# Newton steps of the residual norms moved to GpSimd, and two modulation chunks tied to the second norm of layer 1

## The chip, the cores and the metric

The kernel runs on one core of a Trainium2 chip. The metric is the device time of one execution in microseconds. The core's engines work side by side, each through its own queue in order: TensorE (PE, its weight loads shown apart as PEld), VectorE (DVE), ScalarE (ACT), GpSimd (POOL), and SyncE (SP), which here issues the loads from memory.

## The reference, cut to what matters

Two transformer stacks of two layers each run one after the other on 256 tokens of width 1024, all in float32. The first stack (with a second stream of 256 context tokens) has adaptive layer norms: six modulation vectors per layer come out of a product of the condition with `w_ada`. The change touches the root-mean-square norms and when two parts of that product run:

```python
def rms_norm(x, g):
    xf = x.astype(jnp.float32)
    y = xf * lax.rsqrt(jnp.mean(xf * xf, axis=-1, keepdims=True) + NORM_EPS)
    return (y * g.astype(jnp.float32)).astype(x.dtype)

def adaln(cond, w_ada, b_ada):
    m = jax.nn.silu(cond) @ w_ada + b_ada
    return jnp.split(m, 6, axis=-1)
```

In a layer of the first stack the residual after attention is normed, scaled and shifted by modulation vectors, and goes through a gated feed-forward, `(silu(h @ w_gate) * (h @ w_up)) @ w_down`.

## The kernel before

Activations lie transposed, channels on the 128 partitions in eight tiles (k = 0 to 7) and tokens along the free axis, 256 for each stream. Every float32 weight block of 128 x 128 is split into a rounded part (`whi`, a cast on ScalarE, L210) and a residual (`wlo`, a subtraction on VectorE, L211), the activations likewise (names ending in h and l), and `mm3` makes three matmuls of each product (L336 to L338).

Weights come through a ring of three raw buffers of 1 MB each (tag `raw`), loaded from SP's queue: L203 for the split weights, L487 for modulation weights, which are used unsplit. A load can be issued only when a buffer has been released: a split weight's by its last residual, a chunk's by its matmuls. The loads of SP's queue are issued in order.

A modulation chunk is one of the 12 parts of a layer's `w_ada`: `ada_chunk(l, c)` issues two loads, makes the matmuls of both halves (L494; the second half's buffer is read first), copies the result (L503), transposes it (L505) and reduces it on VectorE (L508, L509). The matmuls are built in `together`, which raises their priority by 3000 and makes the first of them follow the chunk's loads in the planned order. The chunks (1,10) and (1,11) are built behind the modulation of layer 1's second norm, but being of high priority they are planned as soon as their loads allow.

A residual norm goes as follows. The output projection (L336 to L338 into `dn`) adds to the residual stream tile by tile (L711), each tile is squared (L384) and added up (L388). `sum_cols` sums over the partitions with two matmuls against ones (L357), `mean_eps` makes the mean (L362), and `rsqrt` finds the inverse root: two integer instructions for a first guess (L345, L346) and three Newton rounds of three instructions (L348 to L350), all on VectorE with 2 elements in each partition (4 in one case). `spread` turns the result into a row over all partitions with two transposes (L369), ScalarE copies it (L523 or L933), and the modulation (L535 to L537) or the split of the activations follows.

`rsqrt` is called for: the first norm of all (L794), `norm_row` for both streams in layer 0's feed-forward norm, for both at the end of layer 0, and for the one stream in layer 1's feed-forward norm, `row_stats` twice at the start of the layers of the second stack (L917 on), the head norms (`head_rms`), and the final norm. `row_stats` at its first call has 4 columns.

Around the second norm of layer 1 the order of work is: the output projection in two parts, the column sums, the norm, and the feed-forward's first pair of weights (four column groups of 24 matmuls each, 96 in all). A planner sets the order on each engine from priorities, dependencies and its estimates of durations; on the chip each engine keeps that order. A dependency of class NoSync sets the order only.

Of the kernel before, what the change touches and what calls it, by code (L numbers as in the profile page):

```python
# [13 lines left out]
ALU = mybir.AluOpType  # L14
# [4 lines left out]
P = 128  # L19
KT = 8  # L20
D = 1024
# [234 lines left out]
class Build:  # L256
# [82 lines left out]

    def rsqrt(self, v, n, name):  # L340

# [3 lines left out]
        nc.vector.tensor_scalar(y.bitcast(I32), v.bitcast(I32), 1, None, op0=ALU.logical_shift_right)  # L345
        nc.vector.tensor_scalar(y.bitcast(I32), y.bitcast(I32), -1.0, float(0x5F376800), op0=ALU.mult, op1=ALU.add)  # L346
        for _ in range(3):
            nc.vector.tensor_tensor(t, y, y, op=ALU.mult)  # L348
            nc.vector.scalar_tensor_tensor(t, t, -0.5, v, op0=ALU.mult, op1=ALU.mult)
            nc.vector.scalar_tensor_tensor(y, t, 1.5, y, op0=ALU.add, op1=ALU.mult)  # L350
        return y

    def sum_cols(self, acc, n, ps=None):

        ps = self.bank("tr") if ps is None else ps
        for j in range(n):
            self.link(self.nc.tensor.matmul(ps[:, j:j + 1], acc[:, j * P:(j + 1) * P], self.ones, start=True, stop=True))  # L357
        return ps[:, :n]
# [6 lines left out]
    def spread(self, r, n):  # L365

        ps = self.bank("tr")
        for j in range(n):
            self.link(self.nc.tensor.transpose(ps[:, j * P:(j + 1) * P], r[:, j:j + 1].to_broadcast([P, P]), self.ident))  # L369
        return ps[:, :n * P]  # L370
# [97 lines left out]

    def ada_chunk(self, l, c, tag="mm"):

        raws, loads = self.ada_load(l, c, self.wp, "raw", self.raw_bufs)
        ps = self.bank(tag)
        with self.together(loads) as add:
            for i in (1, 0):
# [44 lines left out]
    def norm_row(self, s):  # L519

        rb = self.acc[:, s * 256:s * 256 + 256]
        v = self.mean_eps(self.sum_cols(rb, 2), 2, D, "ms")
        self.nc.scalar.copy(rb, self.spread(self.rsqrt(v, 2, "rn"), 2))  # L523
        return rb
# [211 lines left out]
    def block1(self, ctx):  # L736
# [61 lines left out]
        for l in range(2):  # L798
# [48 lines left out]
            with tc.tile_pool(name=f"ffn{l}", bufs=1, reuse_waits="tile") as fp:  # L847
                h = self.parts(fp, "F")
                for st in apart:
# [8 lines left out]
                    self.modulate(h, self.norm_row(st[0]), l, 1, st[0])  # L858
                    for a in self.ada_gap[l]:
                        self.ada_chunk(*a)  # L860
                f0 = 0
# [53 lines left out]
    def row_stats(self, acc, first):  # L915
# [3 lines left out]
        if first is None:  # L919
            r = self.rsqrt(self.mean_eps(self.sum_cols(acc, 2), 2, D, "ms2"), 2, "rr")  # L920
        else:
# [5 lines left out]
            nc.vector.scalar_tensor_tensor(v[:, 2:4], self.sum_cols(acc, 2), 1.0 / D, t, op0=ALU.mult, op1=ALU.add)  # L927
            r = self.rsqrt(v, 4, "r4")
            r1, r = r[:, 0:2], r[:, 2:4]
# [351 lines left out]
```

## Time and profile before

| | us |
|---|---|
| median of 3 runs | 1557.29 (1557.05 to 1558.81) |
| the profiled execution | 1557.46 |
| its span, first to last instruction | 1555.7 |
| mean granted clock of TensorE in the span | 0.991 |
| TensorE busy | 1498.9 |
| VectorE busy | 1003.9 |
| ScalarE busy | 800.9 |
| GpSimd busy | 67.2 |

Busy times are sums over the span; the ends of matmuls are modelled. The clock is given as a share of the full 2.4 GHz.

### The profile page before, as it was taken

Reading aid. Unit: us, or ns where it says so; the run is one execution under the profiler, and the core shown is the slowest. Engines: PE = TensorE matmul, PEld = TensorE weight load, DVE = VectorE, ACT = ScalarE, POOL = GpSimd, SP = SyncE. Lnnn points to the kernel's source line nnn. Section 1 sums busy time; section 2 is a strip of 40 time slices with the busy share of each in tenths; the row PEclk is TensorE's granted clock in tenths of the full one; section 3 lists DMA queues with packets and bytes.
Section 4 is the critical chain, followed back from the end, with each engine's and each line's share of the span. In section 5 each row is a group of like instructions: output and inputs, shape, how many; then the busy total and the mean of one; then the engine's idle time right before and its main releaser. Section 6 shows DMA issues by size and latency. Waiting matters only on the chain.

```text
span 1555.7 us, 25050 instructions
## 1 busy us (share of the span) xinstructions
PE 1498.9 (96%) x9826; PEld 1291.0 (83%) x9826; DVE 1003.9 (65%) x2210; ACT 800.9 (51%) x1499; POOL 67.2 (4%) x83
## 2 busy tenths in 40 slices
PE   5999999999999999999899999999999999999997
PEld 2776689787788789856599999898899999899996
DVE  4674688333233336867565556898767779987775
ACT  3466665222222224567554445677665456776542
POOL 0200000000000000010000000102100010201000
PEclk9999999999999999999999999999999999999998
DMA  9313355424322524353845554434435544334451
GB/s 370 122 55 115 138 200 187 162 86 158 135 92 98 190 81 139 132 212 109 308 166 189 181 175 168 153 111 160 153 127 184 178 149 156 136 109 163 164 175 42
DMA packets 36982, 238.36 MB, mean 153 GB/s; under 512 B 4224, under 2 KB 5888, under 8 KB 15104
## 3 DMA queue, kind: packets, MB, share of 16 engines
q1 hardware_dynamic: 36576, 236.14, 42.9%
q8 instruction: 77, 1.26, 0.3%
q0 software_dynamic: 288, 0.62, 0.2%
q14 instruction: 41, 0.34, 0.1%
HBM read 236.32 MB, written 1.05 MB: 153 GB/s over the span
## 4 chain that ended last, share of the span: by engine, by line
PE 82%; DVE 10%; ACT 3%; DMA 2%; issue 2%; POOL 0%; SPq 0%; ACTq 0%; POOLq 0%; DVEq 0%
PE mm L336 11%; PE mm L337 10%; PE mm L338 10%; PE g L337 6%; PE g L336 6%; PE g L338 6%; PE dn L337 5%; PE dn L338 5%; PE dn L336 5%; DVE wlo L211 3%; PE mm L494 2%; PE tr L632 2%; PE pv L640 2%; PE pv L996 1%; PE mx L336 1%
## 5 line engine op out<-in xcount | busy, mean ns | idle before, releaser
L210 ACT CAST whi<-raw 128x1024 fp32r<-128x1024 f32 (+4 forms) x392 | 370.0, 949 | 495.3 <-PE mm L337 137.5
L211 DVE TENSOR_TENSOR wlo<-raw,whi 128x1024 fp32r<-128x1024 f32 (+4 forms) x392 | 431.1, 1104 | 198.1 <-ACT whi L210 196.3
L337 PE MATMUL dn<-Hl,whi 128*128 128x256 f32 (+1 forms) x520 | 161.7, 311 | 0.0
L338 PE MATMUL dn<-Hh,wlo 128*128 128x256 f32 (+1 forms) x520 | 161.1, 310 | 0.1
L336 PE MATMUL dn<-Hh,whi 128*128 128x256 f32 (+1 forms) x520 | 160.7, 310 | 0.0
L336 PE MATMUL mm<-Hh,whi 128*128 128x256 f32 (+1 forms) x512 | 149.4, 292 | 1.0 <-DVE mod L508 0.7
L338 PE MATMUL mm<-Hh,wlo 128*128 128x256 f32 (+1 forms) x512 | 150.0, 293 | 0.0
L337 PE MATMUL mm<-Hl,whi 128*128 128x256 f32 (+1 forms) x512 | 149.4, 292 | 0.0
L336 PE MATMUL mm<-whi,Hh 128*128 128x384 f32 (+2 forms) x352 | 129.2, 367 | 0.0
L338 PE MATMUL mm<-whi,Hl 128*128 128x384 f32 (+2 forms) x352 | 127.3, 362 | 0.0
L337 PE MATMUL mm<-wlo,Hh 128*128 128x384 f32 (+2 forms) x352 | 127.2, 361 | 0.0
L336 PE MATMUL mm<-Fh,whi 128*128 128x256 f32 (+1 forms) x368 | 123.0, 334 | 1.7 <-ACT Fh L536 1.7
L338 PE MATMUL g<-Fh,wlo 128*128 128x256 f32 (+1 forms) x368 | 123.0, 334 | 0.3 <-DVE wlo L211 0.3
L336 PE MATMUL g<-Fh,whi 128*128 128x256 f32 (+1 forms) x368 | 122.5, 333 | 0.0
L337 PE MATMUL g<-Fl,whi 128*128 128x256 f32 (+1 forms) x368 | 122.4, 333 | 0.0
L337 PE MATMUL mm<-Fl,whi 128*128 128x256 f32 (+1 forms) x368 | 122.2, 332 | 0.0
L338 PE MATMUL mm<-Fh,wlo 128*128 128x256 f32 (+1 forms) x368 | 122.2, 332 | 0.0
L337 PEld LDWEIGHTS dn<-Hl,whi 128*128 128x128 f32 x520 | 99.1, 191 | 8.3 <-issue 2.5
L338 PEld LDWEIGHTS dn<-Hh,wlo 128*128 128x128 f32 x520 | 99.1, 191 | 6.0 <-issue 0.8
L336 PEld LDWEIGHTS dn<-Hh,whi 128*128 128x128 f32 x520 | 99.0, 191 | 5.6 <-ACT whi L210 0.4
L336 PEld LDWEIGHTS mm<-Hh,whi 128*128 128x128 f32 x512 | 97.9, 191 | 2.2 <-ACT whi L210 0.8
L338 PEld LDWEIGHTS mm<-Hh,wlo 128*128 128x128 f32 x512 | 97.9, 191 | 1.6 <-issue 0.8
(284 smaller groups left out, 3240.2 us busy)
## 6 DMA issues: line engine op xcount, KB each, us to landing
raw<-in_w_ada_dram SPq DMA_DIRECT2D x48, 1024.0 KB, 4.9
raw<-in_w_gu_dram SPq DMA_DIRECT2D x44, 1024.0 KB, 4.9
raw<-in_w_mix_dram SPq DMA_DIRECT2D x32, 1024.0 KB, 4.8
raw<-in_w_in_dram SPq DMA_DIRECT2D x40, 768.0 KB, 4.3
raw<-in_w_in_dram SPq DMA_DIRECT2D x20, 1024.0 KB, 4.8
raw<-in_w_dn_dram SPq DMA_DIRECT2D x16, 1024.0 KB, 4.8
raw<-in_w_dn_dram SPq DMA_DIRECT2D x12, 768.0 KB, 4.3
raw<-in_w_out_dram SPq DMA_DIRECT2D x8, 1024.0 KB, 4.9
```

What stands on the lines that cost most here:

```text
L210: nc.scalar.copy(hi[:, :m], x)
L211: nc.vector.tensor_tensor(lo[:, :m], x, hi[:, :m].bitcast(F32), op=ALU.subtract)
L336: self.link(nc.tensor.matmul(out, lhs[0], rhs[0], start=start, stop=False))
L337: self.link(nc.tensor.matmul(out, lhs[0], rhs[1], start=False, stop=False))
L338: self.link(nc.tensor.matmul(out, lhs[1], rhs[0], start=False, stop=stop))
L494: made.append(self.nc.tensor.matmul(ps[32 * g:32 * g + 32, :], self.s32[:, 4 * i + g, :], raws[i][:, 512 * g:512 * g + 512], start=i == fi ...
L632: nc.tensor.transpose(ps[:, (2 * j + qt) * P:(2 * j + qt + 1) * P], p[i][:, qt, c:c + P], self.ident)
L640: first(nc.tensor.matmul(pv[i * 64:i * 64 + 64, :256], v, pts[i][0][:, j * 256:j * 256 + 256], start=b == 0 and j == 0, stop=b == nk // 2 ...
L996: f(nc.tensor.matmul(pv[64 * i:64 * i + 64, c], vs[i][j], pt[:, d], start=first and j == 0, stop=last and j == 1))
```

## The change

`rsqrt` gets a flag `aside`. With it the first guess stays on VectorE, and the three Newton rounds go to GpSimd, four instructions each instead of three, as GpSimd does the product with v and the step -0.5 x + 1.5 one after the other. `norm_row` and `row_stats` set the flag, which makes seven calls: both streams of layer 0's feed-forward norm, both at the end of layer 0, layer 1's feed-forward norm, and both layers of the second stack.

`sum_cols` and `spread` keep their last matmul and transpose in `self.summed` and `self.turned`. `ada_chunk` takes further instructions that the first of its matmuls has to follow in the order; in layer 1, chunk (1,10) follows the last column sum and chunk (1,11) the last transpose.

```diff
-    def rsqrt(self, v, n, name):
+    def rsqrt(self, v, n, name, aside=False):
...
+        if aside:
+            for _ in range(3):
+                nc.gpsimd.tensor_tensor(t, y, y, op=ALU.mult)
+                nc.gpsimd.tensor_tensor(t, t, v, op=ALU.mult)
+                nc.gpsimd.tensor_scalar(t, t, -0.5, 1.5, op0=ALU.mult, op1=ALU.add)
+                nc.gpsimd.tensor_tensor(y, y, t, op=ALU.mult)
+            return y
         for _ in range(3):
...
-            self.link(self.nc.tensor.matmul(ps[:, j:j + 1], acc[:, j * P:(j + 1) * P], self.ones, start=True, stop=True))
+            self.summed = self.nc.tensor.matmul(ps[:, j:j + 1], acc[:, j * P:(j + 1) * P], self.ones, start=True, stop=True)
+            self.link(self.summed)
...
-            self.link(self.nc.tensor.transpose(ps[:, j * P:(j + 1) * P], r[:, j:j + 1].to_broadcast([P, P]), self.ident))
+            self.turned = self.nc.tensor.transpose(ps[:, j * P:(j + 1) * P], r[:, j:j + 1].to_broadcast([P, P]), self.ident)
+            self.link(self.turned)
...
-    def ada_chunk(self, l, c, tag="mm"):
+    def ada_chunk(self, l, c, tag="mm", after=()):
...
-        with self.together(loads) as add:
+        with self.together(loads + list(after)) as add:
...
-        self.nc.scalar.copy(rb, self.spread(self.rsqrt(v, 2, "rn"), 2))
+        self.nc.scalar.copy(rb, self.spread(self.rsqrt(v, 2, "rn", True), 2))
...
-                    for a in self.ada_gap[l]:
-                        self.ada_chunk(*a)
+                    for a, behind in zip(self.ada_gap[l], (self.summed, self.turned)):
+                        self.ada_chunk(*a, after=[behind])
...
-            r = self.rsqrt(self.mean_eps(self.sum_cols(acc, 2), 2, D, "ms2"), 2, "rr")
+            r = self.rsqrt(self.mean_eps(self.sum_cols(acc, 2), 2, D, "ms2"), 2, "rr", True)
...
-            r = self.rsqrt(v, 4, "r4")
+            r = self.rsqrt(v, 4, "r4", True)
```

## Rows read from the trace of the kernel before

**Rows 1.** The page, part 1: busy us, share of the span, instructions

```profile
PE 1498.9 (96%) x9826; PEld 1291.0 (83%) x9826; DVE 1003.9 (65%) x2210; ACT 800.9 (51%) x1499; POOL 67.2 (4%) x83
```

**Rows 2.** Windows: stretch, length, busy us and count by engine, PE's clock, DMA

```profile
25.00:30.00 5.00, 1.12 (x5) 0.70 (x5) 3.94 (x11) 2.65 (x5) 0.00 (x0) 0.73 1.01 419
...
770.00:775.00 5.00, 2.11 (x17) 1.64 (x16) 4.29 (x12) 3.94 (x6) 0.00 (x0) 0.98 0.90 380
775.00:780.00 5.00, 0.37 (x2) 0.29 (x2) 4.28 (x12) 1.55 (x2) 0.00 (x0) 0.50 1.01 342
780.00:785.00 5.00, 3.48 (x17) 3.19 (x16) 4.27 (x11) 3.04 (x7) 0.00 (x0) 0.50 0.22 92
```

**Rows 3.** Timeline of PE around layer 1's second norm: start, duration us, line, tiles

```profile
760.91 1.92 PE L494 MATMUL mm<-raw,s 128*32 128x512 f32 x16 [0.36 <-DMA raw<-in_w_ada_dram]
...
767.51 1.92 PE L494 MATMUL mm<-raw,s 128*32 128x512 f32 x16
...
769.58 0.28 PE L338 MATMUL dn<-Hh,wlo 128*128 128x256 f32 x1
...
770.29 0.28 PE L338 MATMUL dn<-Hh,wlo 128*128 128x256 f32 x1
...
772.97 0.60 PE L357 MATMUL tr<-ones,acc 128*128 128x1 f32 x4 [1.96 <-DVE acc L388]
...
779.63 0.66 PE L369 MATMUL tr<-ident,rn 128*128 128x128 f32 x2 [5.56 <-DVE rn L350]
...
781.81 0.58 PE L336 MATMUL mm<-Fh,whi 128*128 128x256 f32 x1 [1.52 <-ACT Fh L536]
...
782.41 0.42 PE L336 MATMUL mm<-Fh,whi 128*128 128x256 f32 x1
782.62 0.41 PE L337 MATMUL mm<-Fl,whi 128*128 128x256 f32 x1
```

**Rows 4.** Timeline of SP's queue in the same stretch: issues of loads

```profile
762.03 0.33 SPq L487 DMA_DIRECT2D raw<-in_w_ada_dram  x1
762.89 0.33 SPq L203 DMA_DIRECT2D raw<-in_w_gu_dram  x1
...
768.63 1.19 SPq L203 DMA_DIRECT2D raw<-in_w_gu_dram  x2
```

**Rows 5.** Timeline of VectorE and ScalarE in the same stretch

```profile
771.36 1.22 DVE L211 TENSOR_TENSOR wlo<-raw,whi 128x1024 fp32r<-128x1024 f32 x1
...
772.50 0.42 DVE L388 TENSOR_TENSOR acc<-acc,sq 128x256 f32<-128x256 f32 x1
...
773.51 1.99 ACT L210 CAST whi<-raw 128x1024 fp32r<-128x1024 f32 x2 [0.49 <-DMA raw<-in_w_gu_dram]
...
776.00 1.04 ACT L210 CAST whi<-raw 128x1024 fp32r<-128x1024 f32 x1 [0.50 <-DMA raw<-in_w_gu_dram]
```

**Rows 6.** Timeline: Newton steps in layer 0's norm, and GpSimd's smallest product

```profile
252.04 0.16 DVE L348 TENSOR_TENSOR rn_t<-rn 128x2 f32<-128x2 f32 x1
...
253.60 0.16 DVE L350 SCALAR_TENSOR_TENSOR rn<-rn_t,rn 128x2 f32<-128x2 f32 x1
...
6.17 0.20 POOL L768 TENSOR_TENSOR g<-vec 128x8 f32<-128x8 f32 x1 [4.22 <-DMA vec<-in_vec_dram]
```

**Rows 7.** Timeline of GpSimd and VectorE where both work, near 209 us

```profile
209.08 0.82 DVE L211 TENSOR_TENSOR wlo<-raw,whi 128x640 fp32r<-128x640 f32 x1
209.16 0.93 POOL L730 TENSOR_TENSOR tq<-c,row 128x64 f32<-128x64 f32 x1 [102.42 <-DMA row<-in_row_dram]
...
210.06 0.32 POOL L730 TENSOR_TENSOR tk<-c,row 128x64 f32<-128x64 f32 x1
```

**Rows 8.** Timeline of PE at the spread before the second stack's second layer

```profile
1264.54 0.36 PE L336 MATMUL mm<-whi,Hh 128*128 128x452 f32 x1
1264.73 0.36 PE L337 MATMUL mm<-wlo,Hh 128*128 128x452 f32 x1
1265.19 0.40 PE L369 MATMUL tr<-ident,rr 128*128 128x128 f32 x2
```

## The prediction

> **What bounds the kernel now.** I read the busy shares first: the tensor engine works in 96% of the span, VectorE in 65%, GpSimd in 4% [rows 1]. So nearly everything that keeps PE's queue from moving costs its own length, and what is taken off VectorE or put on GpSimd costs nothing unless PE ends up waiting for it. Next I looked for the stretch where PE is not busy. The windows by stage show one inside the kernel [rows 2]: between 770 and 785 us PE works 2.11, 0.37 and 3.48 us out of 5.00 each, and its granted clock stands at 0.50, the lower of its two levels (1.2 GHz instead of 2.4), from about 775 to 785. This is the second norm of layer 1. The timeline of PE there [rows 3] gives its parts: the two modulation chunks (1,10) and (1,11) run at 760.91 and 767.51 in the middle of the output projection, the projection's last product starts at 770.29, the column sums of the norm at 772.97, the spread at 779.63, the first product of the feed-forward at 781.81. The other six norms that the change touches sit in stretches where PE is always busy; there only a late spread can cost anything.
>
> **Chunks in layer 1's gap: the path shortens.** In the order before, the two chunks stand ahead of the sums. Each holds PE for 1.92 us, and the first waited 0.36 us for its load: 2 x 1.92 + 0.36 = 4.2 us [rows 3]. With the new dependencies chunk (1,10) may only follow the last column sum and chunk (1,11) only the last transpose of the spread, so the projection's last product starts near 766.1. The sums follow it by 2.7 us today, of which some 0.9 us is the addition L388 waiting behind a weight residual of 1.22 us on VectorE [rows 5]; that weight would not yet be loaded (next part), so the wait goes. Sums: 772.97 - 4.2 - 0.9 = 767.9; end of the sums near 768.5.
>
> **The load ring: what is late next.** The raw buffers are three, and feed-forward weights come through them behind the chunks. Rows of SP's queue show the chain [rows 4]: the fourth chunk load is issued at 762.03, when half of the first chunk is multiplied, the first feed-forward load at 762.89, at its end; the next two at 768.63 and 769.49 (two issues of 0.33 us within 1.19), at half and end of the second chunk. So holding the chunks holds these loads, and everything behind them on SP's queue. Chunk (1,10) would now run 768.5 to 770.4. The fourth chunk load is issued near 769.5, the first feed-forward load near 770.4. For two loads issued 0.86 us apart the rows of casts give the landing: the loads of 768.63 and 769.49 released their casts at 773.51 and 776.00, 4.9 and 6.5 us later [rows 4, 5]. Hence the chunk's load lands at 774.4, the feed-forward weight at 776.9, its cast takes 1.0 us, two of them 1.99 [rows 5], and the first feed-forward product can start at 778.0. The norm's own chain must be done before that: 768.5, three VectorE instructions of 0.2 ahead of the steps [rows 6], twelve Newton instructions on GpSimd 2.4 to 2.9 (below), and from the spread to the first product the 2.2 us of today, 779.63 to 781.81 [rows 3]: about 774. The weight, not the norm, ends last, with 4 us to spare, which hides GpSimd's part here. Chunk (1,11) runs 774.4 to 776.3, in PE's wait, and frees the loads for the third and fourth column group: landing 4.9 us after 775.4 is 780.3, both casts and the first residual done near 782.6. The first two groups hold PE for 48 products x 0.12 us (six spacings between 769.58 and 770.29 [rows 3]) = 5.8 us, to 783.8, so that is just covered; if the cover fails, each us of delay is a us lost.
>
> **What it is worth.** The first weight pair is 96 products. Before: 15 of them started by 785.0 at half clock (17 instructions in that window, two of them transposes), 81 remained at 0.12 us, end 794.7 [rows 2, 3]. After, at full clock: 778.0 + 96 x 0.12 = 789.5. That is 5.2 us. **Clock:** it fell about 4 us after the projection's last dense work, with two short bursts of 0.6 us between, and at the start of the kernel too, where PE was busy 1.12 us of 5.00 [rows 2]. After the change the longest thin stretch is 770.4 to 774.4, with only the spread in it. No row shows whether chunks of 1.92 us suffice to hold the clock. Bounds: nothing lost, or the 15 products at 0.21 instead of 0.12 twice over, 2.7 us [rows 3]. I take one such spell, 15 x 0.09 = 1.4 us, since the nearest row, the present gap, shows a fall after a stretch no emptier. Gap: -5.2 + 1.4 = -3.8 us.
>
> **Newton steps on GpSimd.** Seven calls lose 9 VectorE instructions each and gain 12 on GpSimd, because the fused instruction becomes two. On VectorE alone the nine take 252.04 to 253.76, 1.7 us, 0.19 us each [rows 6]; taking 63 of them away is worth nothing by itself, VectorE being in no path there. The smallest GpSimd product on record, 128x8, took 0.20 us [rows 6]; for 128x2 I take 0.20 to 0.24, so a chain of 2.4 to 2.9 us undisturbed. What comes on top is the wait for VectorE: a GpSimd product of 128x64 that began 0.08 us after a residual took 0.93 us, and the same form without neighbour 0.32 [rows 7]: it was held until the residual had finished, 0.6 us. Residuals and additions of that kind stand in VectorE's queue in five norms (not in layer 0's feed-forward norm of the second stream, nor now in layer 1's). PE is in order: the spread's transposes have a fixed place, and behind them queue the products that PE could otherwise run; the row copy of ScalarE and the modulations wait for the transposes, but with slack. Today PE waits only about 0.25 us there: products at 1264.54 and 1264.73, transposes at 1265.19, where 0.20 would be the spacing [rows 8]. Bounds for the five together: -1.2 us (all of today's waits gone) to +8 us (each chain 0.7 longer than nine VectorE steps, plus a hold of 0.6 to 1.2, 1.6 us x 5). I take +0.4 us: the present order meets the end of such a chain within some 0.3 us [rows 8], so the planner's times are good, and the GpSimd chain leaves a VectorE queue in which the steps had to take turns with residuals anyhow. Both ends stay in the range.
>
> A rule speaks against the move. The Trainium skill, Perfetto Trace Analysis, Optimizing Scalar/DVE Operations, says that GpSimd and VectorE share an SBUF read port, held as a lock by a two-port VectorE instruction, so that moving work between the two might not help. By that rule the +8 end would be the nearer one; [rows 7] agree that such holds exist, but not how often twelve small steps meet one.
>
> **Sum.** Profiled execution: 1557.46 us (span 1555.70, 1.76 around it; the median of the runs is 1557.29). 1557.46 - 3.8 + 0.4 = **1554.1 us**.
>
> **Rivals.** (a) The gap stays weight-bound: PE's order puts products of the third or fourth column group early, as the mixed order before does, and PE waits for their residual at 782.6. Then only about 24 products are done by then, 72 remain: end 791.2 at full clock, 2.0 more with the clock low; gain 1.4 to 3.4, less 0.4: near 1556. For it: the buffers hold only three loads and the new waits stand at the head of SP's queue. Against: the order is planned with the landing times in view, and the first chunk waited only 0.36 us for its load today [rows 3]. (b) **Slower:** PE waits for GpSimd. In the five norms whose spread stands among dense products the transposes come into PE's queue where an undisturbed chain would end, while VectorE's residuals hold GpSimd. At 1.6 us each the loss is 8 us: 1557.46 - 3.8 + 8 = 1561.7. It decides from 0.75 us a norm on, where 5 x 0.75 eats the gap's 3.8. For it: [rows 7], and PE's 96%. Against: GpSimd has nothing else to do before the chain, being busy 4% of the span [rows 1], and VectorE's nine steps met the same residuals in their own queue. (c) The hold does not act as told: the chunk's load is late, the clock falls as before and the feed-forward starts at half clock near 781: 1557, no change.
>
> **How the numbers follow.** A change under 0.2% (3.1 us) can't be told from none here. Forecast, the gap gained and the other norms neutral: 0.42, with a range of its own of 1551.0 to 1554.3. Rivals (a) and (c), and mild forms of (b): 0.32, within 3.1 us. Rival (b) in full: 0.26. The range reaches from the gap at full clock with today's waits gone, 1557.46 - 5.2 - 1.2 = 1551.0, to (b), 1561.7.
>
> **What would show it.** Right: in the trace after, both chunks lie between the sums and the first feed-forward product, sums near 768, first product near 778, landing of a weight as its releaser. The clock around 775 tells the 1.4 us. Wrong: PE idle ahead of the transposes, released by GpSimd, of 1 us or more in the layer-0 norms, at 980 or at 1265; GpSimd steps of much over 0.25 us spacing; PE waiting for a residual inside the first weight pair; an extra loss in the output projection, if something other than the chunks held it.

## The result and the profile after

| | before | after |
|---|---|---|
| median of the runs shown | 1557.29 us (1557.05 to 1558.81) | 1580.0 us (1573.95 to 1580.79) |
| ratio | | 1.0127, 95% interval 1.0116 to 1.0138 |
| profiled execution, span | 1557.46 us, 1555.70 us | 1574.94 us, 1573.2 us |

The change makes the kernel 1.3% slower; 1554.1 us was forecast, with a range up to 1561.7. The runs of after lie in two groups, near 1574 us (mean granted clock 0.988 and 0.991) and near 1580 us (0.986 and 0.987); the profile is of the first, and no trace here shows the second. The ratio is not the quotient of the two medians, which is 1.0146; that of the means of the runs shown is 1.0131.

The page's part 1, to be held against [rows 1] (busy us, share of the span, instructions):

```profile
PE 1504.6 (96%) x9826; PEld 1294.0 (82%) x9826; DVE 997.0 (63%) x2147; ACT 801.1 (51%) x1499; POOL 88.3 (6%) x167
```

VectorE is 6.9 us less busy, GpSimd 21 us more, and PE's work grew by 5.7 us with the same 9826 instructions, which points to stretches at the lower clock. The difference of the spans, 17.5 us, is mostly time in which PE stood still (17.5 less 5.7: 11.8 us). The waits of PE say for whom (who <- for whom: us in total, times, longest):

```profile
PE tr L377 <- POOL rn L352: 10.8, 5, 4.2
PE tr L377 <- DVE rr L940: 4.2, 2, 2.6
```

L377 are the spread's transposes, L352 is the last instruction of a Newton round on GpSimd, and L940 is VectorE's small copy behind the steps in the second stack. In before the transposes waited more than 0.1 us in one norm of these seven, layer 1's [rows 3]. The timeline of PE at the seven norms (start, us, engine, line, operation, tiles; in brackets the idle time before and what ended it), the first with its column sums:

```profile
231.28 0.61 PE L364 MATMUL tr<-ones,acc 128*128 128x1 f32 x4
...
236.98 0.69 PE L377 MATMUL tr<-ident,rn 128*128 128x128 f32 x2 [2.12 <-POOL rn L352]
...
259.25 0.43 PE L377 MATMUL tr<-ident,rn 128*128 128x128 f32 x2 [1.37 <-POOL rn L352]
...
627.49 0.43 PE L377 MATMUL tr<-ident,rn 128*128 128x128 f32 x2 [2.33 <-POOL rn L352]
...
649.73 0.62 PE L377 MATMUL tr<-ident,rn 128*128 128x128 f32 x2 [4.18 <-POOL rn L352]
...
786.48 0.43 PE L377 MATMUL tr<-ident,rn 128*128 128x128 f32 x2 [0.84 <-POOL rn L352]
...
997.99 0.40 PE L377 MATMUL tr<-ident,rr 128*128 128x128 f32 x2 [1.63 <-DVE rr L940]
...
1281.95 0.40 PE L377 MATMUL tr<-ident,rr 128*128 128x128 f32 x2 [2.56 <-DVE rr L940]
```

The seven waits sum to 15.0 us. GpSimd's own rows show the steps, undisturbed at 256 us and held at 644 us:

```profile
255.97 0.19 POOL L349 TENSOR_TENSOR rn_t<-rn 128x2 f32<-128x2 f32 x1 [19.04 <-DVE rn L346]
...
259.00 0.19 POOL L352 TENSOR_TENSOR rn<-rn,rn_t 128x2 f32<-128x2 f32 x1
...
643.88 1.50 POOL L349 TENSOR_TENSOR rn_t<-rn 128x2 f32<-128x2 f32 x1 [16.45 <-DVE rn L346]
645.46 1.45 POOL L350 TENSOR_TENSOR rn_t<-rn_t,ms 128x2 f32<-128x2 f32 x1
```

From the first start to the twelfth are 3.03 us, 0.275 us a step, though a row shows 0.19 of work; the undisturbed chain of twelve takes 3.2 us. The two held steps lie beside VectorE's weight residuals of 1.22 us:

```profile
644.11 1.22 DVE L211 TENSOR_TENSOR wlo<-raw,whi 128x1024 fp32r<-128x1024 f32 x1
...
645.64 1.22 DVE L211 TENSOR_TENSOR wlo<-raw,whi 128x1024 fp32r<-128x1024 f32 x1
```

The decisive comparison is how much work stands between the column sums and the transposes in PE's queue. From the starts of the two, less the wait (before: [rows 8] and the same view of the other norms; layer 1's apart):

| norm, before at | before: work | after: work | after: wait |
|---|---|---|---|
| 230.34 to 237.30 | 6.96 | 3.58 | 2.12 |
| 250.62 to 255.25 | 4.63 | 4.40 | 1.37 |
| 614.13 to 620.02 | 5.89 | 3.82 | 2.33 |
| 632.74 to 639.14 | 6.40 | 3.45 | 4.18 |
| 977.69 to 983.03 | 5.34 | 5.08 | 1.63 |
| 1261.16 to 1265.19 | 4.03 | 2.92 | 2.56 |

Twelve steps that take longer than the nine they replace have **less** work ahead of the transposes than before. The planner that fixes the order brought the transposes forward in all six norms, by 0.2 to 3.4 us of work.

The longer chain and this move both count. From the sums to the transposes after took 5.7, 5.8, 6.2, 7.6, 6.7 and 5.5 us. With the work of before still ahead of the transposes, the same chains would have left waits of 0, 1.1, 0.3, 1.2, 1.4 and 1.4 us. That is some 5.5 of the 14.2 us that these six norms wait; the other 8.7 come from the move forward. This split is an estimate from the table; no run made it.

PE's stops cost clock as well. Windows of after (stretch, length, busy us by engine, PE's granted clock as a share of 2.4 GHz, DMA):

```profile
235.00:240.00 5.00, 3.02 (x14) 3.02 (x15) 2.38 (x7) 1.81 (x4) 1.43 (x7) 0.68 0.39 162
...
650.00:655.00 5.00, 5.00 (x17) 4.00 (x16) 4.21 (x11) 3.00 (x7) 0.00 (x0) 0.68 0.00 0
```

In before the clock is full in both places; 5 x 0.32 = 1.6 us each.

**The account by stage.** I took the distance between the same ScalarE instruction in after and in before, stage by stage: +6.3 us over layer 0's feed-forward norms (230 to 280), +8.3 over the norms at the end of layer 0 (614 to 660), -1.2 near 700 (a load, explained under the run with GpSimd's steps in layer 1's second norm alone), -0.7 over layer 1's second norm, +1.5 at 980, +2.6 at 1262, and 0.9 that is there from 40 us on: 17.7. The waits and the clock account for 3.5 + 1.6 of the first and 6.5 + 1.6 of the second. Of the 1.2 us left in the first, 0.9 are two waits of PE for casts of ScalarE, between the two norms; in before PE waits 0.46 us in this stage, after 1.37 beside the transposes:

```profile
245.91 0.39 PE L336 MATMUL mm<-Fh,whi 128*128 128x256 f32 x1 [0.59 <-ACT whi L210]
...
249.21 0.38 PE L336 MATMUL g<-Fh,whi 128*128 128x256 f32 x1 [0.78 <-ACT whi L210]
```

**The gap of layer 1.** The timeline of PE in after, answering to [rows 3]:

```profile
781.91 0.61 PE L364 MATMUL tr<-ones,acc 128*128 128x1 f32 x4 [1.54 <-DVE acc L397]
782.45 3.19 PE L503 MATMUL mm<-raw,s 128*32 128x512 f32 x16
...
788.85 1.92 PE L503 MATMUL mm<-raw,s 128*32 128x512 f32 x16 [1.50 <-DMA raw<-in_w_ada_dram]
...
794.52 0.39 PE L336 MATMUL mm<-Fh,whi 128*128 128x256 f32 x1 [1.79 <-ACT whi L210]
```

The hold acts as told: the chunks (L503) lie behind the sums and behind the transposes. With the 14.3 us by which this stage comes later taken off, sums, transposes and first product stand at 767.6, 772.2 and 780.2; before they stood at 772.97, 779.63 and 781.81. Of 5.4 us at the sums 1.6 are left at the first product. PE's clock is 0.80, 0.86, 1.00 and 0.66 in the four stretches of 780 to 800. The first product waits for the weight's cast, and that is late mostly because the weight is: its load is issued at 785.69 and lands 7.5 us later, at 793.1 or 793.2, and the cast begins at 793.44, behind the last two of the second stream's modulation (L545) in ScalarE's queue. The load in the view of transfers (size, us from issue to landing) and ScalarE's timeline:

```profile
raw<-in_w_gu_dram SPq DMA_DIRECT2D x1, 1024.0 KB, 7.5
```

```profile
792.62 0.91 ACT L545 ACTIVATE Fh<-nt,mod 128x256 fp32r<-128x256 f32 x2 [0.60 <-DVE nt L544]
793.44 1.98 ACT L210 CAST whi<-raw 128x1024 fp32r<-128x1024 f32 x2
```

### The profile page after: what moved, and what is told of

Read it like the earlier page. It is cut to its first block, busy times and chain, and to the rows that moved or that the text cites. A ratio compares the mean times of both kernels' runs of the same rounds, so it can differ in the third digit from the quotient of the medians.

```text
span 1573.2 us, 25078 instructions
## 1 busy us (share of the span) xinstructions
PE 1504.6 (96%) x9826; PEld 1294.0 (82%) x9826; DVE 997.0 (63%) x2147; ACT 801.1 (51%) x1499; POOL 88.3 (6%) x167
## 4 chain that ended last, share of the span: by engine, by line
PE 83%; DVE 9%; ACT 3%; issue 2%; POOL 2%; DMA 1%; SPq 0%; DVEq 0%; ACTq 0%; POOLq 0%
PE mm L336 10%; PE mm L337 10%; PE mm L338 10%; PE g L337 6%; PE g L336 6%; PE g L338 6%; PE dn L337 5%; PE dn L338 5%; PE dn L336 5%; DVE wlo L211 3%; PE mm L503 2%; PE tr L641 2%; PE pv L649 2%; PE pv L1005 1%; PE mx L336 1%
```

## The experiments

**Theory:** the loss comes from the transposes' place in PE's queue, ahead of the end of GpSimd's chain; the hold gains a little. **Rivals:** the hold itself loses the time (load ring, clock); GpSimd's steps lose it wherever the transposes stand, by their own length and by VectorE's holds. Ratios are against the kernel before, timed on the same chip.

### The hold alone

```diff
-        self.nc.scalar.copy(rb, self.spread(self.rsqrt(v, 2, "rn", True), 2))
+        self.nc.scalar.copy(rb, self.spread(self.rsqrt(v, 2, "rn"), 2))
```

and the same for the two calls in row_stats.

> The two chunks are held as in the changed kernel, all Newton steps stay on VectorE. Theory (the loss of 17.5 us comes from the Newton steps alone, PE waiting at seven spreads; the hold by itself gives back 0.7 us in the changed kernel's trace): 0.5 to 3 us below the kernel before, about 1555.5, because nine VectorE steps (1.8 us) replace a GpSimd chain of 3.3 us in the gap. Rival (the hold itself costs, as the feed-forward's loads wait for the chunks): 1558 to 1562.

Measured: 0.9993 (0.9983 to 1.0002). PE's timeline and the windows:

```profile
767.12 0.61 PE L364 MATMUL tr<-ones,acc 128*128 128x1 f32 x4 [1.55 <-DVE acc L397]
767.65 3.20 PE L503 MATMUL mm<-raw,s 128*32 128x512 f32 x16
770.78 0.69 PE L377 MATMUL tr<-ident,rn 128*128 128x128 f32 x2
...
774.20 2.94 PE L503 MATMUL mm<-raw,s 128*32 128x512 f32 x16 [2.00 <-DMA raw<-in_w_ada_dram]
...
779.62 0.58 PE L336 MATMUL mm<-Fh,whi 128*128 128x256 f32 x1 [0.62 <-ACT whi L210]
```

```profile
765.00:770.00 5.00, 3.45 (x25) 1.41 (x24) 3.20 (x15) 0.50 (x2) 0.00 (x0) 0.81 0.01 2
770.00:775.00 5.00, 2.92 (x18) 0.99 (x18) 3.17 (x9) 2.51 (x6) 0.00 (x0) 0.84 0.97 320
775.00:780.00 5.00, 3.63 (x18) 1.32 (x10) 4.27 (x14) 3.88 (x8) 0.00 (x0) 0.50 1.04 328
780.00:785.00 5.00, 4.85 (x23) 4.55 (x22) 3.94 (x4) 3.55 (x4) 0.00 (x0) 0.50 0.84 306
```

The hold costs nothing and is worth next to nothing: sums 5.9 us earlier than in before, the first product 2.2 us (0.7 of each is won near 700 already), and the stage as a whole 0.15 us. PE's clock falls already before 770, where it was full nearly up to 775 [rows 2]; the chunks take 3.20 and 2.94 us for 1.92, the second waits 2.00 us for its load, and the first products run at the half clock up to 785. The 1.3% are not the hold's.

### The Newton steps alone

```diff
-                    for a, behind in zip(self.ada_gap[l], (self.summed, self.turned)):
-                        self.ada_chunk(*a, after=[behind])
+                    for a in self.ada_gap[l]:
+                        self.ada_chunk(*a)
```

> The Newton steps of all seven norms on GpSimd, the chunks not held. Theory (the loss is that of the Newton steps): 17 to 20 us above the kernel before, 1574 to 1577 in its quicker executions, with PE idle ahead of the transposes, released by GpSimd, of some 15 us in all. Rival (a good part of the loss comes from the hold): at most 10 us above, 1567.

Measured: 1.0143 (1.0127 to 1.0159). The loss is that of the Newton steps: the span is 21.3 us longer than in before, a little more than the 17 to 20 expected. Without the hold layer 1's gap loses as well, 2.6 us by the account by stage: the transposes wait there 0.3 us longer than in before (5.56 [rows 3]), the first product comes 0.6 us later behind the sums, and the clock is at 0.88, 0.50, 0.50 and 0.75 in the four stretches of 785 to 805. In the last of them PE is busy throughout, so that 0.75 costs it some 1.2 us; in before the clock is full again from 785. The stage at 1262 loses 3.8 us where it lost 2.6 in after, with the clock at 0.87 and 0.78 behind the wait. The transposes of layer 1's gap:

```profile
793.58 0.69 PE L377 MATMUL tr<-ident,rn 128*128 128x128 f32 x2 [5.89 <-POOL rn L352]
```

### The transposes later in PE's queue

The whole change, with the priority of the spread's transposes lowered by 150 places:

```diff
     def spread(self, r, n):
         ps = self.bank("tr")
+        self.tc.cur_priority += 150
         for j in range(n):
...
+        self.tc.cur_priority -= 150
```

> The whole change, and the transposes of every spread get a lower priority (150), so that the planner puts 74, 45, 92, 25, 50 and 53 products between the column sums and the transposes of the six dense norms, where the changed kernel has 24, 32, 26, 12, 22 and 11 and the kernel before 52, 27, 43, 26, 23 and 16. Theory (the chain on GpSimd is not too long for the kernel, the transposes only stand too early in PE's queue): nearly the whole loss goes, 1555 to 1560, and PE's waits for GpSimd ahead of the transposes fall from 15 us to under 3. Rival (GpSimd steps cost by holding VectorE's residuals and casts, wherever the transposes stand): still 1568 or more.

Measured: 1.0006 (0.9997 to 1.0015). All steps are still on GpSimd, and its holds are there (0.65 and 0.84 us at 233.47 and 235.08, 1.45 twice at 636.49 and 638.02), but the work between sums and transposes is now 9.4 us in the first norm (230.19 to 239.60) and 10.8 in the last (1264.31 to 1275.10), and two waits are left:

```profile
641.19 0.43 PE L378 MATMUL tr<-ident,rn 128*128 128x128 f32 x2 [1.72 <-POOL rn L352]
...
774.19 0.69 PE L378 MATMUL tr<-ident,rn 128*128 128x128 f32 x2 [1.24 <-POOL rn L352]
```

So the place of the transposes decides most of the loss: by stage the six norms lose 3.9 us here (0.6, 2.2, 1.3 and -0.2) for 18.7 in after. GpSimd's length and holds cost little while dense work covers them, but not nothing: 1.72 us is the wait that is left at 641, in the norm with the two holds of 1.45, and in two stages PE has a wait of 1 us that after has not:

```profile
259.34 0.39 PE L336 MATMUL mm<-Fh,whi 128*128 128x256 f32 x1 [1.09 <-ACT Fh L547]
...
986.81 0.44 PE L336 MATMUL mm<-whi,Hh 128*128 128x384 f32 x1 [1.03 <-ACT v L967]
```

The ratio also has the 1.2 us near 700 in it, which this run wins like after. VectorE's relief brings nothing that can be seen: no norm's stage gains more than 0.2 us.

### Two rounds on GpSimd

The whole change with `range(2)` for `range(3)` in GpSimd's loop; the third round of every residual norm is left out.

> Edit: the whole change, with two rounds of Newton on GpSimd instead of three; the third round of every residual norm is left out. Theory (the transposes stand too early in TensorE's queue, since the order counts a GpSimd step for less than it takes): eight steps in place of twelve take 4 x 0.274 = 1.10 us less, and the transposes are moved forward by only 2 to 3 products (0.24 to 0.36 us) in four of the norms and by 10 in one, so TensorE's waits at the transposes (2.12, 1.37, 2.33, 4.18, 0.84, 1.63, 2.56 us, sum 15.0) fall by 0.7 to 0.9 us each where nothing else moves, some 4.6 us in all, and the ratio from 1.0127 to 1.0097 (1.008 to 1.0105). Rival 1 (the loss lies in the changed order itself or in VectorE's hold of single steps): the waits stay as they are, ratio 1.012 to 1.014. Rival 2 (the order follows the number of steps at their real price): the transposes move forward by the 9 products that 1.10 us are, and nothing changes either; told apart from rival 1 by the count of products ahead of the transposes.

Measured: 1.0070 (1.0057 to 1.0084). The waits at the transposes fell from 15.0 to 8.84 us (1.39, 0.64, 1.59, 2.45, 0.16, 0.75, 1.86), for example:

```profile
236.36 0.43 PE L377 MATMUL tr<-ident,rn 128*128 128x128 f32 x2 [1.39 <-POOL rn L352]
```

In the first three norms they fell by 0.73, 0.73 and 0.74, where 0.7 to 0.9 was expected: four steps take 1.10 us, while the work ahead of the transposes shrank by only 0.36, 0.34 and 0.35 us (three products of 0.12), that is 0.09 us a step. In these norms the order reckons with a third of what a step takes. It isn't so in all: at 980 the work shrank by 2.0 us, ten products. In the fourth norm the second of the two held steps fell from 1.45 to 0.32 us besides.

The ratio fell by more than expected (1.0097), and that is not explained by the waits: the spans of the two traces, 1573.2 and 1571.7 us, differ by 1.5 us only, though the waits differ by 6.2. In this run's trace PE waits 3.10 us for a chunk's load at 276.43 (0.12 in after) and has the clock at 0.66 behind it. So the waits at the transposes are this run's evidence, not its ratio.

### The hold, and GpSimd's steps in layer 1's second norm alone

```diff
-    def norm_row(self, s):
+    def norm_row(self, s, aside=False):
...
-                    self.modulate(h, self.norm_row(st[0]), l, 1, st[0])
+                    self.modulate(h, self.norm_row(st[0], l == 1), l, 1, st[0])
```

with `aside` handed on to rsqrt, and not set in row_stats.

> The chunks held, and the Newton steps on GpSimd only in layer 1's second norm; the other six stay on VectorE. Theory: the six other norms carry the whole loss, so this one is 0.3 to 2 us below the kernel before, 1555.3 to 1557; against the kernel with the hold alone it is 0 to 2 us longer, since the GpSimd chain in this norm takes 1.5 us more. Rival (the loss in layer 1's gap is hidden by an offset that the earlier norms cause): 1560 or more.

Measured: 0.9987 (0.9977 to 0.9996). Faster by 0.1%, but not by what was tested: in the trace the gap's stage loses 0.2 us, and the span is 0.8 us shorter because of 1.1 us won in another place, at a chunk in layer 1's attention whose load was late in before. The same chunk in the traces of before and of this run:

```profile
700.59 1.92 PE L494 MATMUL mm<-raw,s 128*32 128x512 f32 x16 [1.11 <-DMA raw<-in_w_ada_dram]
```

```profile
699.52 1.92 PE L503 MATMUL mm<-raw,s 128*32 128x512 f32 x16
```

The load took 6.4 us from issue to landing in before and 5.1 here. It is so in all traces: 4.8 to 5.1 us and no wait in the eight with GpSimd's steps in layer 1's second norm, 5.8 to 6.9 us and a wait of 0.52 to 1.62 us in before and the five with all steps on VectorE. One thing differs ahead of this chunk. GpSimd's queue also issues a load of 352 KB, `mk`, for the second stack, in before at 689.02, and it lands 7.2 us later, while the chunk's load (694.14 to 700.55) is under way. With the Newton steps in that queue it stands behind them. GpSimd's timeline in before and in this run:

```profile
689.02 0.60 POOL L1219 DMA_DIRECT2D mk<-in_c_dram  x1
```

```profile
770.96 0.60 POOL L1228 DMA_DIRECT2D mk<-in_c_dram  x1
```

It is issued at 689 in the six traces with the late chunk and at 771 to 793 in the eight others. So this gain is most likely an effect of the steps' move after all, far from the norm; no run moved that load alone. A ratio within 0.1% of 1 therefore says nothing of the gap, and the stage does.

### Own buffers for the second chunk

On top of the last: chunk (1,11) takes its loads into two buffers of the feed-forward pool instead of the ring of three.

```diff
-        raws, loads = self.ada_load(l, c, self.wp, "raw", self.raw_bufs)
+        raws, loads = self.ada_load(l, c, room, "raw4", 2) if room else self.ada_load(l, c, self.wp, "raw", self.raw_bufs)
...
-                        self.ada_chunk(*a, after=[behind])
+                        self.ada_chunk(*a, after=[behind], room=fp if a == (1, 11) else None)
```

> Edit: as the run with the hold and GpSimd's Newton steps in layer 1's second norm alone, and chunk (1,11) takes its two loads into buffers of their own in the feed-forward pool instead of into the ring of three that it shares with the weights. Theory (load ring): in that earlier run the second chunk waits for its load (0.70 us, at 773.32), the first feed-forward weight is loaded behind it (issued at 769.58, landing 7.1 us later), and the first feed-forward product comes at 779.46 behind the weight's cast. With the ring free, chunk (1,11) starts right behind the transposes (771.1 + 0.5 = 771.6), takes 3.2 to 3.6 us at the half clock, and the first product comes at 775 to 776: 3.5 to 4.5 us less, a ratio against the kernel before of 0.9960 (0.9950 to 0.9970). Rival 1 (clock and modulation): the weight is there, but the second stream's modulation, which takes VectorE 6.4 us from 772.2 in the earlier run, now shares VectorE with the weights' residuals (1.2 us each) and the second stream's products wait for it: ratio 0.998 or more, and PE waits at Fh or Fl behind the 96 products of the first stream. Rival 2 (the second weight load binds): it is issued behind the first chunk as before, lands at about 777, and the third and fourth column groups wait 1 to 2 us: 0.9970 to 0.9980.

Measured: 0.9977 (0.9968 to 0.9987). The second chunk no longer waits for a load, and the first product comes at 775.81 as worked out, but the gap's stage gains 2.1 us instead of 3.5 to 4.5. The number alone would fit rival 2 as well (0.9970 to 0.9980; the second weight load landed at 776.4). The trace speaks for rival 1: VectorE is busy for all of 775 to 785, and the residual that PE waits for at 778.46 starts at 777.19 behind VectorE's part of the modulation, though its cast was done at 775.5. In the windows and in PE's timeline:

```profile
770.00:775.00 5.00, 3.39 (x18) 0.69 (x18) 2.52 (x5) 3.06 (x7) 1.69 (x7) 0.75 0.91 377
775.00:780.00 5.00, 3.55 (x27) 3.07 (x24) 5.00 (x12) 4.32 (x8) 0.00 (x0) 0.91 0.54 108
```

```profile
778.46 0.38 PE L338 MATMUL g<-Fh,wlo 128*128 128x256 f32 x1 [0.95 <-DVE wlo L211]
```

### The same with the steps on VectorE

`self.norm_row(st[0])` for `self.norm_row(st[0], l == 1)`.

> Edit: the same with the Newton steps back on VectorE everywhere, so the hold and the own buffers alone. Theory: from the sums to the transposes the held norm took 771.07 - 766.49 = 4.58 us with GpSimd's steps and 770.78 - 767.12 = 3.66 us with VectorE's, so this is the run before less 0.9 us: ratio 0.9954 if that comes to 0.9960, and in any case 0.0002 to 0.001 lower. Rival: VectorE's nine steps stand in its queue between the last residual and the weights' residuals and cost there what they save: no difference, or 0.0005 higher.

Measured: 0.9991 (0.9982 to 0.9999). Not the 0.0002 to 0.001 less that was expected; the intervals of the two runs overlap, but the sign is the rival's, and the gap's stage loses 0.3 us where it gained 2.1. The transposes come 0.26 us earlier (771.35 for 771.61; with the later start of this run's stage taken off it is the 0.9 that was worked out) and the first product at 775.73, yet PE then waits 0.75, 0.20, 0.26, 0.44 and 1.00 us for wlo, Fh and Fl, and the clock falls to 0.75 and 0.57 in 780 to 790, where it was full with GpSimd's steps. 0.8 us of the difference is the chunk load near 700. The rest may be what GpSimd takes from VectorE in this one stretch, where VectorE is the last. The trace shows a rival: the clock also falls over chunk (1,10), which takes 3.14 us for 1.92, so that the next feed-forward load is issued at 771.46 for 769.54 and lands at 779.2 for 776.4. Neither was tried by itself.

### Own buffers without the hold

`self.ada_chunk(*a, room=...)`, no `after`.

> Edit: the own buffers for chunk (1,11) alone: no hold, all Newton steps on VectorE, so the chunks stand among the output projection's products as in the kernel before. It tells what the hold is worth once the loads don't bind. Theory (the hold fills a wait of TensorE): without it the sums come at about 773, TensorE idles from there through the 3.7 us to the transposes, and the first feed-forward product comes at 776.6 to 777, against 775 to 776 with the hold: ratio 0.9968, that is 0.0005 to 0.001 above the held one, and the clock falls for the idle 3.7 us. Rival (the load ring is all): held or not, the chunks' 2 x 1.92 us are paid once, TensorE's idle time of the norm is hidden in either case by nothing else, and with the loads early this kernel is as fast as the held one or faster, since TensorE stays at the full clock through the chunks (1.92 us each against 3.2 to 3.6 us): ratio equal within 0.0004 or lower.

Measured: 0.9995 (0.9987 to 1.0004). The sums come at 772.45, the transposes wait 5.52 us as before, and the first product is at 782.06, not at 776.6 to 777; the gap's stage loses 0.6 us. Freeing the ring alone is worth nothing. Against the held run with VectorE's steps the difference is 0.0004, too little to tell what the hold adds.

### The weights' casts ahead of the modulation

Own buffers, hold and GpSimd's steps there, and `self.weights_first = 100` around the first feed-forward weight's WCols in layer 1.

> Edit: as the run with own buffers (ratio 0.9977), with the casts and residuals of the first feed-forward weights put ahead of the second stream's modulation in ScalarE's and VectorE's queues (four casts and four residuals ahead of most of it). Theory (the first stream's 96 products need no modulation of the second, so weights should come first): the waits for wlo at 778.46 (0.95 us) and 783.50 (0.63 us) go, 1 to 1.6 us less: 0.9967 to 0.9971. Rival: the second weight load lands only at about 777, its casts stand ahead of the modulation, Fh starts at 779 and takes 6.4 us, and the second stream's products, due 11.5 us behind the first at some 787, wait: 0.9977 to 0.9985.

Measured: 0.9992 (0.9983 to 1.0000), the rival's side and beyond (the gap's stage loses 1.0 us). The transposes wait 2.97 us where they waited 2.13, as the early residuals hold GpSimd's last step (1.04 us at 772.01). Then the casts of the second load start at 778.19 and stand in ScalarE's queue ahead of the modulation, whose Fh starts at 780.09, and PE waits for that:

```profile
780.65 0.46 PE L336 MATMUL mm<-Fh,whi 128*128 128x256 f32 x1 [1.64 <-ACT Fh L545]
```

### TensorE kept busy in the gap: hold alone, hold with own buffers, own buffers alone

The edit, with 12 and 8, 12 and 16, and 12 and 24 products whose results nobody reads, ahead of the column sums and between them and the transposes:

```diff
+    def filler(self, n, behind):
+        ps = self.bank("dn")
+        for _ in range(n):
+            ins = self.nc.tensor.matmul(ps[:, :256], self.ident_r, self.idle_rhs, start=True, stop=True)
...
+            behind = ins
+        return behind
```

> Edit: the hold alone (Newton steps on VectorE), and 20 more TensorE products of 128x256 whose results nobody reads, placed where TensorE stood idle in the run with the hold alone: 12 between the output projection's last product and the column sums (1.55 us of idle time), 8 between the held chunk and the transposes. Theory (the clock takes back what the hold saves): in that run the granted clock was 0.81 in 765 to 770 and 0.84, 0.50, 0.50 in the three stretches of 5 us after it, and chunk (1,10) took 3.20 us in place of 1.92. With TensorE kept busy the chunk takes 1.92 us, the ring's buffers come free 1.3 us earlier, so the second chunk's load and the feed-forward weight too; the first feed-forward product comes at 778 to 778.6 in place of 779.6, and if the clock then also holds through 775 to 785, its products save up to 2.8 us: ratio against the kernel before 0.9970 to 0.9985, against 0.9993 for the hold alone. Rival 1 (the loads bind, the clock doesn't matter): the first product stays at 779.6, ratio 0.9993 as before or, since 20 products x 0.12 = 2.4 us are added that may not fit the idle time, up to 1.001. Rival 2: the clock falls later, in the stretch 772 to 779 that isn't filled, and only the 1 us of the chunk is won: 0.9987.

Measured: 0.9989 (0.9980 to 0.9998), the second rival's 0.9987: the clock is full up to 775, chunk (1,10) takes 1.92 us, but the second chunk's load is issued hardly earlier (769.10 for 769.19, the sums standing 0.3 us later), the chunk waits longer (2.59 for 2.00), and behind that wait the clock falls, to 0.54 and 0.50 in 775 to 785. The gap's stage gains 0.3 us. The first product is at 779.35.

```profile
774.26 2.61 PE L516 MATMUL mm<-raw,s 128*32 128x512 f32 x16 [2.59 <-DMA raw<-in_w_ada_dram]
```

> Edit: the run with the hold, GpSimd's steps in layer 1's second norm alone and own buffers for chunk (1,11) (ratio 0.9977), with 12 such products ahead of the sums and 16 between the held chunk and the transposes, where TensorE waited 1.55 and 2.13 us. Theory (clock): the granted clock was 0.75 in 770 to 775 and 0.91 in 775 to 780; the second chunk took 3.14 us in place of 1.92. At the full clock chunk and transposes come 1.2 to 1.7 us earlier: ratio 0.9966 to 0.9970. Rival (VectorE binds there): VectorE was busy for all of 775 to 785 with the modulation and the weights' residuals, and TensorE waited for wlo, Fh and Fl at 778.46, 781.29, 781.97 and 783.50; then an earlier chunk is answered by a longer wait there and the ratio stays at 0.9977.

Measured: **0.9956** (0.9944 to 0.9969), 1552.7 us beside 1559.62 for the kernel before: below the expected 0.9966, which the interval still holds, and the fastest of all kernels here, ahead of before and after. The clock is full throughout:

```profile
767.91 1.93 PE L516 MATMUL mm<-raw,s 128*32 128x512 f32 x16
...
772.81 0.43 PE L388 MATMUL tr<-ident,rn 128*128 128x128 f32 x2 [0.95 <-POOL rn L361]
773.17 1.92 PE L516 MATMUL mm<-raw,s 128*32 128x512 f32 x16
...
776.06 0.36 PE L344 MATMUL mm<-Fh,whi 128*128 128x256 f32 x1 [0.38 <-DVE mod L530]
```

```profile
770.00:775.00 5.00, 4.05 (x34) 2.27 (x33) 3.53 (x5) 3.83 (x6) 2.76 (x8) 1.00 0.98 367
775.00:780.00 5.00, 3.67 (x31) 3.22 (x28) 4.30 (x10) 4.88 (x9) 0.00 (x0) 1.00 0.98 300
```

The gap's stage gains 5.0 us; 1.2 more are the chunk load near 700 again. The clock is only a part of the 2.9 us that this run is ahead of the one without the products. The second chunk takes 1.92 us for 3.14, yet the first product comes hardly earlier (776.06 for 775.81, in a stage that starts some 0.4 us later). The larger part lies behind it, where PE's waits fell from 2.8 to 1.0 us, and there the order differs too: with the products in it the first weight's casts stand ahead of the row copy and the modulation in ScalarE's queue, where they stood behind the row copy. ScalarE's first cast here and in the run without the products:

```profile
770.38 2.00 ACT L210 CAST whi<-raw 128x1024 fp32r<-128x1024 f32 x2
```

```profile
772.35 1.05 ACT L210 CAST whi<-raw 128x1024 fp32r<-128x1024 f32 x1
```

So the products kept the clock up and changed the order of other engines; which of the two brought how much isn't shown. The rival (VectorE binds, nothing is won) did not come true: a wait for Fl of 0.96 us at 777.50 is what is left of it.

> Edit: no hold and no GpSimd steps (the chunks among the output projection's products as before), own buffers for chunk (1,11), and the products whose results nobody reads: 12 ahead of the column sums and 24 behind them, where TensorE waited 1.96 and 5.52 us. It tells whether the clock and the buffers alone bring what the run with hold, buffers and filled idle time brought (ratio 0.9956), so whether the hold has a part in it. Theory (the hold has a part): unheld, the sums come at 772.5 instead of 767.4, the transposes 3.7 to 7 us behind them, and TensorE's useful work stands still meanwhile whatever the clock; the first feed-forward product comes at 778 to 781 at the full clock, against 776.1: ratio 0.9970 to 0.9990. Rival (clock and buffers do it all): first product by 777, ratio 0.9950 to 0.9962, and the hold is worth nothing.

Measured: 0.9994 (0.9985 to 1.0003), just above the worse end expected with a part for the hold (0.9990); 0.9 us is won in the stage. The clock is full up to 780 (0.66 in 780 to 785), but PE still waits 2.64 us ahead of the transposes (779.34) and the first product is at 781.27. That the hold has a part in the 5.0 us is likely, as the sums come 5.3 us later here (772.72 for 767.38). It isn't shown, because this run lacks GpSimd's steps as well, and those made a difference of 2.4 us between the two runs with hold and own buffers (2.1 won and 0.3 lost). What is shown: hold, buffers, products and GpSimd's steps together bring 5.0 us; hold and buffers 2.1 with the steps and -0.3 without, hold and products 0.3, buffers and products 0.9.

## Why the prediction was wrong

**The step that failed: "+0.4 us" for the Newton steps.** By stage they cost 6.3 + 8.3 + 1.5 + 2.6 = 18.7 us outside layer 1. The sentence "the planner's times are good" carried it. It was read off one spread that met its chain within 0.3 us [rows 8]; that was a chain of VectorE's steps, and it was carried over to GpSimd's, of which the trace had no such chain. The order put 2.9 to 5.1 us of work ahead of the transposes where the way from the sums to the transposes, with VectorE's instructions and all twelve steps in it, took 5.5 to 7.6. The run with late transposes (18.7 us down to 3.9) and the waits of the one with two rounds show it from both sides.

**The bounds were too narrow.** The +8 us assumed 1.6 us in each of five norms, as if the transposes stood where they stood before; by the estimate above that would have cost some 5.5 us of waits, within the bound, and the other 8.7 come from their move forward. All six lost, and the waits were 1.37 to 4.18 us. Three sizes were off: a step was put at 0.20 to 0.24, from the duration of GpSimd's smallest product [rows 6], and what counts is the distance from start to start, 0.275; the second stream's norm in layer 0 was left out as free of holds, which it was, and still waited 1.37; the last stream's norm at the end of layer 0 had two steps of 1.50 and 1.45 us, 2.6 us of hold where 0.6 to 1.2 was allowed. And two of the stops (2.12 and 4.18 us) had the clock at 0.68 behind them, 1.6 us each, which no step reckoned with; those of 2.33 and 2.56 us had it full.

**Rival (b) named the mechanism** (PE waits for GpSimd at the transposes, decided from 0.75 us a norm) and had 0.26; its argument against, that VectorE's steps met the same residuals, was beside the point, as the transposes' place was not the same. The Trainium skill (Perfetto Trace Analysis, Optimizing Scalar/DVE Operations) has the shared read port as the reason why moving work between the two engines might not help. The held steps of 0.67 to 1.50 us agree with it, but the run with late transposes has them too and loses 3.9 us in place of 18.7: here the holds decided part of the size.

**Right:** PE at 96% bounds the kernel, and taking 63 instructions off VectorE was worth nothing. The hold acts as the code says, and with the hold alone the sums came at 767.12 (767.9 forecast), the fourth chunk load was issued at 769.19 and the first feed-forward load at 770.90 (769.5 and 770.4 forecast); 0.7 us of these times is won near 700.

**The gap's -3.8 us was -0.7 in after and -0.15 with the hold alone.** The first product came at 780.2 in after (14.3 us taken off) and at 779.6 with the hold alone, not at 778.0. Of the 2.2 us in after, 1.0 is the weight's load, issued at 771.4 for 770.4, as chunk (1,10) ran at the lower clock and took 3.19 us for 1.92; another 1.0 is its way to the landing, 7.5 us for 6.5; and 0.3 is the cast, which stood behind the second stream's modulation in ScalarE's queue (0.5 with the hold alone), a queue that the step hadn't looked at. The clock term, 1.4 us, was too small as well: with the hold alone the clock fell over the first chunk (0.81 and 0.84 in 765 to 775), then was at 0.50 from 775 to 785 as in before; in after it fell over that chunk and again behind the first product (0.66 in 795 to 800). Rival (c) came nearest: the chunk's load is late and the clock falls, and its price, no change, is what the hold alone measured, though the hold itself acts as told. With own buffers and products that keep PE busy, hold and GpSimd's steps bring 5.0 us in this stage, so the gap was there to be won, but not by the hold alone.

**Left open:** 0.3 us of the first stage, why the ratio with two rounds fell by more than the traces show, and how the 5.0 us divide among hold, GpSimd's steps, clock and changed order.

## What to carry to other kernels

When a chain is moved to another engine, don't ask how long it takes there but what the order assumes it takes: look at how much work stands between its first input and its consumer in the in-order queue, and expect that distance to be wrong for an engine of which the trace has no such instruction. If PE is the bound, put the consumer late: being late (6 to 12 us of work ahead of it) cost about 1 us in two stages here, being early cost up to 4.2 us and the clock. Look also at what else stands in the new engine's queue: the steps pushed back a load there, which is the likely reason why another stage got 1.2 us shorter. A gap in PE's work is worth its length plus the clock behind it. Filling it with products that nobody reads brought the best kernel here, but the order of other engines changed with it, so compare the queues of all engines before giving the clock the credit.

## What the runs showed that I had not expected

- A dependent step of 128x2 on GpSimd takes 0.275 us from start to start, where its row shows 0.19.
- A GpSimd step beside a VectorE residual of 1.22 us takes 1.45 to 1.50 us, and two can follow each other; that chain of twelve took 5.8 us where an undisturbed one takes 3.2.
- A chunk's load in layer 1's attention took 6.4 or 5.1 us from issue to landing depending on which engine does a norm's steps 70 us later. GpSimd's own load of 352 KB was issued at 689 us in the one case and behind the steps in the other.
- Twenty-eight useless products (3.6 us of PE's time) made the kernel faster: with them the clock stayed at 1.00 in 770 to 780 instead of 0.75 and 0.91, the first weight's casts came 2 us earlier, and the ratio went from 0.9977 to 0.9956, though the two intervals (0.9968 to 0.9987, 0.9944 to 0.9969) still touch.
